# Three quarters of a down projection by Strassen's scheme on one core of a Trainium2

## The chip, the cores and the metric

The kernel runs on one core of one Trainium2 chip. The metric is device time in microseconds (us) of the whole program, smaller is better. Engines are named as in the profile: PE (TensorE matmuls), PEld (its weight loads), DVE (VectorE), ACT (ScalarE), POOL (GpSimd), SP (the queue that issues most DMAs).

## What is computed

One encoder block on 512 tokens (and 16 meta tokens) of width 2048: a mixer (short convolution and neighbourhood attention), then a squared-ReLU MLP with 8192 hidden columns. The change lies in the last product of the MLP.

```python
h_res = h_res + mix @ w_out[l]
h = rms_norm(h_res, norm2_g[l])
h_res = h_res + jnp.square(jax.nn.relu(h @ w_up[l])) @ w_down[l]     # (512, 8192) @ (8192, 2048)
out = rms_norm(h_res, final_norm_g)[:, N_META:]
```

All is float32. Every product is made of three float32r matmuls: an operand x is kept as hi + lo (hi is x rounded, lo is x - hi), and x*y is hi*hi + hi*lo + lo*hi.

## The kernel before

Stages in order: input projection with convolution and attention, output projection with the operands of the up projection, up projection, down projection, final norm. Weights come in slabs of 128 x 1024 (512 KB). `load` (L157) takes the next of three buffers named `raw` and issues the DMA on SP; `split` (L180) makes hi by an ACT cast (L182) and lo by a DVE subtraction (L183). SP, ACT, DVE and POOL each work through their instructions in program order, and a `raw` buffer is free again when what was loaded into it has been split.

**Up projection** (L741 to L782). It already goes by the Strassen-Winograd scheme: a product of 2 x 2 blocks with seven block products (table `PROD`) in place of eight. There are 32 outputs n (256 hidden columns each), four steps s for each n, and one slab for each step. A step holds two sums indices m; for each m there are 7 products of 3 matmuls of 128x256, so 42 matmuls in a step, the 21 of the first m ahead of the 21 of the second. The first three products use blocks of the slab as they are (buffers `q`, three of them), the other four use sums of blocks (`tsum`, two buffers, then `wsp`, three buffers). `up_slab` makes these sums on DVE (L747 to L749). The activation operands, seven blocks for each m and each as hi and lo, lie in `places`: m = 0 to 3 in `sobuf`, 4 and 5 in `xa_hi` and `xa_lo`, 6 and 7 in `xc`. `up_out` (L767) joins the products of one n (an ACT copy and six DVE instructions that read PSUM, L774 to L779), applies the squared ReLU on ACT, and writes the result to DRAM (`a_d`).

**Down projection** (L815 to L849). It goes in eight chunks of 1024 hidden rows, and in each chunk over four groups i of 512 output columns. For each i there are 8 x 4 x 3 = 96 matmuls of 128x512 (`mm3`, L632 to L635; 128 tokens stationary, 512 columns of weights moving), four slabs `dn` that are split as they are, and four DVE instructions (L845) that scale a PSUM bank and add it to `acc`. In the first group of a chunk four loads of `a_d` are split into `sobuf` (seven buffers of it).

Of the kernel before, what the change touches and what calls it, by code (L numbers as in the profile page):

```python
# [99 lines left out]
def hybrid_block_kernel(  # L100
# [56 lines left out]
    def load(src, name):  # L157
        raw = wring["raw"].next(name)
        wring["last"] = nc.sync.dma_start(raw, src)
        return raw  # L160
# [209 lines left out]
    xa_hi = xap.tile([P, 8, SEQ], F32R, name="xa_hi")  # L370
    xa_lo = xap.tile([P, 8, SEQ], F32R, name="xa_lo")
# [3 lines left out]
    def xc_tiles(pool, n):  # L375
        for i in range(n):
            f = len(xc2)
            hi = pool.tile([P, 2, SEQ], F32R, name=f"xc_hi{f}")
            lo = pool.tile([P, 2, SEQ], F32R, name=f"xc_lo{f}")
            xc2.append((hi, lo))  # L380
# [4 lines left out]
    with tc.tile_pool(name="at", bufs=1, side="left") as at:  # L385
# [18 lines left out]
        for p in range(NPAIR):  # L404
# [122 lines left out]
            split(xa_hi[:, p, :], xa_lo[:, p, :], o, scale=ag[:, p : p + 1])  # L527
# [89 lines left out]
    places += [[(0, 7, by7(flat(t)[:, :SW7]))] for t in (xa_hi, xa_lo)]  # L617
# [20 lines left out]
    xa = [(xa_hi[:, f, :], xa_lo[:, f, :]) for f in range(8)]  # L638
# [86 lines left out]
    a_d = [dram.tile([P, 4 * HT], F32, name=f"a_d{n}") for n in range(NG)]  # L725
# [15 lines left out]
    def up_slab(n, s):  # L741
        raw = load(w_up[n, s], f"up{n}_{s}")
        w, t = by4(raw), by4(TS.next())
        q_hi, q_lo = (by4(v, 3) for v in Q3.next())
        split(q_hi, q_lo, w[:, :, 1:4, :])
        b12 = free_ap(raw[:, 0:1], [[512, 2], [0, 2], [1, P]])
        nc.vector.tensor_tensor(t[:, :, 0:2, :], b12, w[:, :, 1:3, :], op=ALU.add)  # L747
        nc.vector.tensor_tensor(t[:, :, 2, :], t[:, :, 0, :], w[:, :, 2, :], op=ALU.add)
        nc.vector.tensor_tensor(t[:, :, 3, :], t[:, :, 2, :], w[:, :, 3, :], op=ALU.add)  # L749
        t_hi, t_lo = (by4(v) for v in part_tiles(f"up{n}_{s}"))  # L750
        split(t_hi, t_lo, t)
        return (q_hi, q_lo), (t_hi, t_lo)

    def up_step(bs, n, s):
        both = up_slab(n, s)
        for k in range(2):
            m = 2 * s + k
            for q, (sm, w, x, b, c) in PROD.items():
                o = bs[b][:, c * HT : (c + 1) * HT]
                h, l = (v[:, k, w, :] for v in both[sm])  # L760
                xh, xl = (operand[m][x][:, i, :] for i in range(2))
# [3 lines left out]
                nc.tensor.matmul(o, lhsT=l, rhs=xh, start=False, stop=m == NPR - 1, skip_group_check=True)  # L765

    def up_out(bs, n):  # L767


        e, u = E.next()  # L770
        e, u = (v.rearrange("p (s c) -> p s c", c=HT) for v in (e, u))
# [28 lines left out]
    xcp.release()  # L800
    xe.release()
    xap.release()
    wp2 = ctx.enter_context(tc.tile_pool(name="wp2", bufs=1, side="left"))
    wring["raw"] = Ring(*raw_slots(3, wp), *raw_slots(2, wp2))
    wring["split"] = Ring(*split_slots(3, wp), *split_slots(3, wp2))
    A = Ring(*[lambda name, i=i: part(sobuf, 2048, i) for i in range(7)])
    pf = ctx.enter_context(tc.tile_pool(name="pf", bufs=1, side="left"))
    gF = pf.tile([P, D], F32, name="gF")
    sq = pf.tile([P, NT, 5], F32, name="sq")
    junk = [pf.tile([P, 512], F32, name=f"junk{i}") for i in range(2)]  # L810

    QUART = {(1, 1): 0, (0, 0): 1, (1, 0): 2, (0, 1): 3}
    tags = ["mm", "aux"]
    turn = 0
    for ch in range(NCHUNK):  # L815
# [3 lines left out]
        if last:  # L819
            with tc.issue_after(wring["last"].ins):  # L820
                nc.sync.dma_start(gF, final_g.partition_broadcast(P))
        for i in range(3 if last else 4):
            bs = [bank(tags[turn], f"d{ch}_{i}_{t}") for t in range(NT)]
            turn ^= 1
            for s_ in range(0, FCH, 2):
                if i == 0:

                    n = 4 * ch + s_ // 2
                    both = A.next()
                    split(both[:, 0:1024], both[:, 1024:2048], load(a_d[n], f"a{n}"))  # L830
# [24 lines left out]
    for t in range(NT):  # L855
# [7 lines left out]
        for i in range(halves):  # L863
# [7 lines left out]
            nc.scalar.activation(junk[t % 2][:, :n], a, AF.Square, accum_out=sq[:, t, 3 + i : 4 + i])  # L871
            nc.vector.tensor_tensor(a, a, gF[:, 1536 + i * n : 1536 + (i + 1) * n], op=ALU.mult)
# [6 lines left out]
        for i in range(4):  # L879
# [5 lines left out]
            nc.sync.dma_start(out_v[t][:, :, i * 512 : (i + 1) * 512], o)  # L885

# [58 lines left out]
```

## Time and profile before

| what | value |
| --- | --- |
| median of 3 runs (lowest to highest) | 2155.45 us (2155.43 to 2155.64) |
| profiled execution | 2155.03 us, of which the traced span is 2153.3 us |
| up projection | about 800 to 1447 us of the span |
| down projection without its last group | about 1447 to 2122 us |
| PE busy over the span | 2141.1 us, 99% |

The span runs from the first to the last instruction of the trace. PE's busy time counts overlapping matmuls, so the rate of a stage is read from the distance between the starts of matmuls.

### The profile page before, as it was taken

What the parts mean: (1) busy time and instruction counts of PE and PEld (TensorE: products, weight loads), DVE (VectorE), ACT (ScalarE), POOL (GpSimd) and SP (SyncE); (2) the same over time, 40 slices, a digit from 0 to 9 for tenths busy, and PEclk for the clock granted to TensorE, in tenths of its full rate; (3) what the DMA queues carried; (4) which work ended last, traced back from release to release, by engine and by line L of the source; (5) the groups of instructions that cost most, each with busy time, mean ns of one, the idle gap of its engine ahead of it and who ended that gap; (6) DMA issues with size and microseconds to landing.
All of it is one profiled execution on the core that took longest, in us unless ns stands there. A gap on an engine that the chain in (4) does not pass through costs nothing.

```text
span 2153.3 us, 33207 instructions
## 1 busy us (share of the span) xinstructions
PE 2141.1 (99%) x13660; PEld 1954.4 (91%) x13660; DVE 1291.3 (60%) x2015; ACT 799.4 (37%) x1110; POOL 141.1 (7%) x256
## 2 busy tenths in 40 slices
PE   9999999999999999999999999999999999999998
PEld 8999999999988889999999999998888888888887
DVE  7776766343435569888888888874444343434434
ACT  6455544222212335544544544552222222222223
POOL 1332321001110000000000000000000000000001
PEclk9999999999999999999999999999999999999999
DMA  5332222222253334334334333356343333433422
GB/s 193 91 93 79 77 90 71 97 90 96 91 166 108 118 127 136 131 126 138 130 126 138 131 124 138 133 193 223 114 133 106 126 127 108 137 117 117 147 89 79
DMA packets 89997, 261.32 MB, mean 121 GB/s; under 512 B 25636, under 2 KB 25716, under 8 KB 88692
## 3 DMA queue, kind: packets, MB, share of 16 engines
q1 hardware_dynamic: 84660, 238.22, 33.9%
q10 hardware_dynamic: 4608, 16.78, 1.9%
q0 software_dynamic: 576, 4.19, 0.5%
q8 instruction: 107, 1.75, 0.3%
q14 instruction: 46, 0.38, 0.1%
HBM read 233.99 MB, written 25.17 MB: 120 GB/s over the span
## 4 chain that ended last, share of the span: by engine, by line
PE 98%; POOL 1%; SPq 0%; DMA 0%; ACT 0%; issue 0%; POOLq 0%; ACTq 0%; DVE 0%
PE d L633 10%; PE d L634 10%; PE d L635 10%; PE u L764 10%; PE u L765 10%; PE u L763 10%; PE mm_u L211 1%; PE mm_c L211 1%; PE mm_u L208 1%; PE mm_c L208 1%; PE mm_u L209 1%; PE mm_c L209 1%; PE mm_b L211 1%; PE mm_b L208 1%; PE mm_b L209 1%; PE o_a L635 1%
## 5 line engine op out<-in xcount | busy, mean ns | idle before, releaser
L633 PE MATMUL d<-wsp_dn,sobuf 128*128 128x512 f32 x992 | 385.9, 389 | 0.0
L634 PE MATMUL d<-wsp_dn,sobuf 128*128 128x512 f32 x992 | 385.9, 389 | 0.0
L635 PE MATMUL d<-wsp_dn,sobuf 128*128 128x512 f32 x992 | 385.9, 389 | 0.0
L183 DVE TENSOR_TENSOR wsp_dn<-raw_dn,wsp_dn 128x1024 fp32r<-128x1024 f32 x124 | 151.7, 1224 | 265.7 <-ACT wsp_dn L182 265.5
L182 ACT CAST wsp_dn<-raw_dn 128x1024 fp32r<-128x1024 f32 x124 | 130.7, 1054 | 377.4 <-PE d L635 367.7
L635 PEld LDWEIGHTS d<-wsp_dn,sobuf 128*128 128x128 f32 x992 | 186.2, 188 | 38.7
L633 PEld LDWEIGHTS d<-wsp_dn,sobuf 128*128 128x128 f32 x992 | 186.2, 188 | 38.7
L634 PEld LDWEIGHTS d<-wsp_dn,sobuf 128*128 128x128 f32 x992 | 186.2, 188 | 38.6
L182 ACT CAST q<-raw_up 128x768 fp32r<-128x768 f32 x128 | 106.9, 835 | 236.1 <-PE u L764 167.0
L183 DVE TENSOR_TENSOR wsp_up<-tsum,wsp_up 128x1024 fp32r<-128x1024 f32 x128 | 156.4, 1223 | 49.0 <-ACT wsp_up L182 45.0
L182 ACT CAST wsp_up<-tsum 128x1024 fp32r<-128x1024 f32 x128 | 134.3, 1050 | 69.9 <-PE u L765 64.6
L763 PE MATMUL u<-sobuf,wsp_up 128*128 128x256 f32 x512 | 145.0, 283 | 0.0
L764 PE MATMUL u<-sobuf,wsp_up 128*128 128x256 f32 x512 | 145.0, 283 | 0.0
L765 PE MATMUL u<-sobuf,wsp_up 128*128 128x256 f32 x512 | 144.6, 283 | 0.0
L183 DVE TENSOR_TENSOR q<-raw_up,q 128x768 fp32r<-128x768 f32 x128 | 122.4, 957 | 34.3 <-ACT q L182 34.2
L764 PE MATMUL u<-sobuf,q 128*128 128x256 f32 x384 | 108.7, 283 | 0.0
L763 PE MATMUL u<-sobuf,q 128*128 128x256 f32 x384 | 108.5, 283 | 0.0
L765 PE MATMUL u<-sobuf,q 128*128 128x256 f32 x384 | 108.5, 283 | 0.0
L183 DVE TENSOR_TENSOR sobuf<-raw_a,sobuf 128x1024 fp32r<-128x1024 f32 x32 | 39.2, 1225 | 103.2 <-ACT sobuf L182 103.2
L845 DVE SCALAR_TENSOR_TENSOR acc<-d,few,acc 128x512 f32<-128x512 f32 x124 | 86.2, 749 | 23.9 <-PE d L635 23.9
L763 PEld LDWEIGHTS u<-sobuf,wsp_up 128*128 128x128 f32 x512 | 98.3, 192 | 0.0
L764 PEld LDWEIGHTS u<-sobuf,wsp_up 128*128 128x128 f32 x512 | 98.3, 192 | 0.0
(307 smaller groups left out, 5466.7 us busy)
## 6 DMA issues: line engine op xcount, KB each, us to landing
raw_up<-in_w_up_dram SPq DMA_DIRECT2D x128, 512.0 KB
raw_dn<-in_w_down_dram SPq DMA_DIRECT2D x124, 512.0 KB
a_d<-xq ACTq DMA_DIRECT2D x32, 512.0 KB
raw_a<-a_d SPq DMA_DIRECT2D x32, 512.0 KB
raw_q<-in_w_in_dram SPq DMA_DIRECT2D x16, 512.0 KB
raw_u<-in_w_in_dram SPq DMA_DIRECT2D x16, 512.0 KB
raw_c<-in_w_in_dram SPq DMA_DIRECT2D x16, 512.0 KB
raw_b<-in_w_in_dram SPq DMA_DIRECT2D x16, 512.0 KB
```

What stands on the lines that cost most here:

```text
L182: first = nc.scalar.copy(hi, src)
L183: second = nc.vector.tensor_tensor(lo, src, hi.bitcast(F32), op=ALU.subtract)
L208: nc.tensor.matmul(b, lhsT=wh, rhs=cols(h_hi, kt), start=kt == 0, stop=False)
L209: nc.tensor.matmul(b, lhsT=wh, rhs=cols(h_lo, kt), start=False, stop=False)
L211: last = nc.tensor.matmul(b, lhsT=wl, rhs=cols(h_hi, kt), start=False, stop=kt == KT - 1)
L633: nc.tensor.matmul(o, lhsT=ah, rhs=wh, start=start, stop=False)
L634: nc.tensor.matmul(o, lhsT=ah, rhs=wl, start=False, stop=False)
L635: nc.tensor.matmul(o, lhsT=al, rhs=wh, start=False, stop=stop)
L763: nc.tensor.matmul(o, lhsT=h, rhs=xh, start=first, stop=False, skip_group_check=True)
L764: nc.tensor.matmul(o, lhsT=h, rhs=xl, start=False, stop=False, skip_group_check=True)
L765: nc.tensor.matmul(o, lhsT=l, rhs=xh, start=False, stop=m == NPR - 1, skip_group_check=True)
L845: nc.vector.scalar_tensor_tensor(a, bs[t], rs2[:, t : t + 1], a, op0=ALU.mult, op1=ALU.add)
```

## The change

The first 6144 of the 8192 hidden rows (`NPD` = 24 of the 32 outputs n) go through the down projection in the transposed Strassen form; the last 2048 stay in the old form, as chunks 6 and 7. The new part has four chunks `ch` of 1536 hidden rows (`CP` = 6 sums indices m). In each chunk there are eight groups G of 256 output columns; a group has three steps of one slab and 42 matmuls of 128x256, in which weights are stationary and activations move. So there are 4 x 8 x 3 = 96 steps.

- The sums of weight blocks of these steps are made by POOL instead of DVE (`step_slab` with `nc.gpsimd`): one instruction of 512 elements for each partition and two of 256.
- `up_out` has POOL make four sums of activation blocks (256 elements each) for the first 24 n, and writes them to DRAM too.
- `down_operand` loads the operands of one m in two parts (`da`, 768 columns, and `ds`, 1024 columns), through the same three `raw` buffers, and splits them into `places`, over the operands that were there. It is called inside the last group of the chunk before (and inside n = 31 of the up projection for chunk 0), two m after each step.
- A group ends in `combine_out` (an ACT copy and six DVE instructions). In chunk 0 that writes `accT`; in chunks 1 to 3 it writes a buffer that POOL adds to `accT` (one instruction of 1024 elements).
- In chunk 6 PE transposes `accT` back (64 transposes of 128x128), and 16 more DVE instructions add it to `acc`.

```diff
+    NPD = 24
+    xs = xap.tile([P, 4, HT], F32, tag="xa1", name="xs")
-    def up_slab(n, s):
-        raw = load(w_up[n, s], f"up{n}_{s}")
+    def step_slab(raw, eng, name):
         w, t = by4(raw), by4(TS.next())
         q_hi, q_lo = (by4(v, 3) for v in Q3.next())
         split(q_hi, q_lo, w[:, :, 1:4, :])
         b12 = free_ap(raw[:, 0:1], [[512, 2], [0, 2], [1, P]])
-        nc.vector.tensor_tensor(t[:, :, 0:2, :], b12, w[:, :, 1:3, :], op=ALU.add)
-        nc.vector.tensor_tensor(t[:, :, 2, :], t[:, :, 0, :], w[:, :, 2, :], op=ALU.add)
-        nc.vector.tensor_tensor(t[:, :, 3, :], t[:, :, 2, :], w[:, :, 3, :], op=ALU.add)
+        eng.tensor_tensor(t[:, :, 0:2, :], b12, w[:, :, 1:3, :], op=ALU.add)
+        eng.tensor_tensor(t[:, :, 2, :], t[:, :, 0, :], w[:, :, 2, :], op=ALU.add)
+        eng.tensor_tensor(t[:, :, 3, :], t[:, :, 2, :], w[:, :, 3, :], op=ALU.add)
...
+        if n < NPD:
+            nc.gpsimd.tensor_tensor(xs[:, 0, :], e[:, 0, :], e[:, 1, :], op=ALU.subtract)
+            nc.gpsimd.tensor_tensor(xs[:, 1, :], xs[:, 0, :], e[:, 2, :], op=ALU.subtract)
+            nc.gpsimd.tensor_tensor(xs[:, 2, :], e[:, 2, :], e[:, 0, :], op=ALU.subtract)
+            nc.gpsimd.tensor_tensor(xs[:, 3, :], e[:, 3, :], xs[:, 1, :], op=ALU.add)
+            nc.gpsimd.dma_start(a_d[n][:, 1024:], xs.rearrange("p s c -> p (s c)"))
+    CP = 6
+    def down_operand(n):
+        v = places[n % CP][0][2]
+        r = load(a_d[n][:, 256:1024], f"da{n}", 768)
+        split(v[:, 0:3, 0, :], v[:, 0:3, 1, :], by_q(r))
+        r = load(a_d[n][:, 1024:], f"ds{n}")
+        split(v[:, 3:7, 0, :], v[:, 3:7, 1, :], by_q(r))
...
             up_step(bs, n, s_)
+            if n == NG - 1 and s_ < 3:
+                for m in range(2 * s_, 2 * s_ + 2):
+                    down_operand(m)
         up_out(bs, n)
+    for ch in range(NPD // CP):
+        for G in range(8):
+            bs = banks(G)
+            for s_ in range(CP // 2):
+                name = f"dt{ch}_{G}_{s_}"
+                raw = wring["raw"].next(name)
+                for k in range(2):
+                    wring["last"] = nc.sync.dma_start(
+                        raw[:, k * 512 : (k + 1) * 512].rearrange("p (e c) -> p e c", e=2),
+                        w_down[G // 2, ch * CP + 2 * s_ + k].rearrange("p (e c) -> p e c", e=2)[:, :, G % 2 * 256 :][:, :, :256],
+                    )
+                step(bs, step_slab(raw, nc.gpsimd, name), ops_d, 2 * s_, CP)
+                if G == 7 and ch + 1 < NPD // CP:
+                    for m in range(2 * s_, 2 * s_ + 2):
+                        down_operand((ch + 1) * CP + m)
+            if ch == 0:
+                t = acc_pools[G].tile([P, 2, SEQ], F32, tag=f"xc_{('hi', 'lo')[G % 2]}{G // 2}", name=f"accT{G}")
+                accT.append(by_q(flat(t)))
+                combine_out(bs, accT[G], u_d)
+            else:
+                e = ED.next()
+                combine_out(bs, e, u_d)
+                nc.gpsimd.tensor_tensor(accT[G], accT[G], e, op=ALU.add)
...
-    for ch in range(NCHUNK):
+    for ch in range(first_ch, NCHUNK):
...
+                if ch == first_ch:
+                    pt = bank(tags[turn], f"pt{i}_{t}")
+                    for k in range(4):
+                        v = accT[2 * i + k // 2][:, QUART[t // 2, k % 2], t % 2 * P : (t % 2 + 1) * P]
+                        nc.tensor.transpose(pt[:, k * P : (k + 1) * P], in_=v, identity=ident)
+                    nc.vector.scalar_tensor_tensor(a, pt, rs2[:, t : t + 1], a, op0=ALU.mult, op1=ALU.add)
```

**Where instructions stand.** First SP at the end of the up projection. `raw_up31_1` is the slab of n = 31, step 1; `raw_a0` and `raw_dn0_0_0` are the first activations and weights of the down projection. Before:

```order
L159 DMA raw_up31_0_14773<-in_w_up_dram 128x1024
L159 DMA raw_up31_1_14825<-in_w_up_dram 128x1024
L159 DMA raw_up31_2_14877<-in_w_up_dram 128x1024
L159 DMA raw_up31_3_14929<-in_w_up_dram 128x1024
L159 DMA raw_a0_15012<-a_d0_7855 128x1024
L159 DMA raw_dn0_0_0_15016<-in_w_down_dram 128x1024
```

With the change, where `raw_da0` and `raw_ds0` are the two parts of the operands of m = 0:

```order
L159 DMA raw_up31_0_14895<-in_w_up_dram 128x1024
L159 DMA raw_da0_14947<-a_d0_7856 128x768
L159 DMA raw_ds0_14951<-a_d0_7856 128x1024
L159 DMA raw_da1_14955<-a_d1_7857 128x768
L159 DMA raw_ds1_14959<-a_d1_7857 128x1024
L159 DMA raw_up31_1_14963<-in_w_up_dram 128x1024
L159 DMA raw_da2_15015<-a_d2_7858 128x768
L159 DMA raw_ds2_15019<-a_d2_7858 128x1024
L159 DMA raw_da3_15023<-a_d3_7859 128x768
L159 DMA raw_ds3_15027<-a_d3_7859 128x1024
L159 DMA raw_up31_2_15031<-in_w_up_dram 128x1024
```

Four operand loads now stand between one slab and the next, and the next but one; the three `raw` buffers are taken in this order. SP shows the same pattern (`dt0_7_0`, four operand loads, `dt0_7_1`, four, `dt0_7_2`, four, `dt1_0_0`) at the end of each of chunks 0, 1 and 2.

Second DVE in chunk 0 at its last group, where before stood a slab's subtraction (`wsp_dn`) and the L845 instructions of the old form:

```order
L183 TENSOR_TENSOR sobuf_6589<-raw_ds6_16419,sobuf_6589 128x4x256
L183 TENSOR_TENSOR sobuf_6589<-raw_da7_16423,sobuf_6589 128x3x256
L183 TENSOR_TENSOR sobuf_6589<-raw_ds7_16427,sobuf_6589 128x4x256
L183 TENSOR_TENSOR q3_1_7852<-raw_dt0_7_1_16431,q3_1_7852 128x768
L183 TENSOR_TENSOR wsp_dt0_7_1_16439<-tsum_7851,wsp_dt0_7_1_16439 128x1024
L183 TENSOR_TENSOR sobuf_6589<-raw_da8_16484,sobuf_6589 128x3x256
L183 TENSOR_TENSOR sobuf_6589<-raw_ds8_16488,sobuf_6589 128x4x256
```

The subtractions for the operands of m = 0 and 1 of the next chunk stand ahead of those for the slab of the step that PE does next.

Third POOL in chunk 3 (in the down projection before, POOL had nothing until the final norm), around the sums of group 4:

```order
L750 TENSOR_TENSOR tsum_7851<-raw_dt3_4_0_20097 128x2x256
L751 TENSOR_TENSOR tsum_7851<-tsum_7851,raw_dt3_4_0_20097 128x2x128
L752 TENSOR_TENSOR tsum_7851<-tsum_7851,raw_dt3_4_0_20097 128x2x128
L750 TENSOR_TENSOR tsum_7851<-raw_dt3_4_1_20150 128x2x256
L860 TENSOR_TENSOR accT2_15666<-accT2_15666,xq_6617 128x1024
L751 TENSOR_TENSOR tsum_7851<-tsum_7851,raw_dt3_4_1_20150 128x2x128
```

The three sums of each slab and, once in a group, the addition to `accT` of two groups ago follow each other on POOL.

## Rows read from the trace of the kernel before

**Rows 1.** The page: busy time by engine, and the chain that ended last.
```profile
PE 2141.1 (99%) x13660; PEld 1954.4 (91%) x13660; DVE 1291.3 (60%) x2015; ACT 799.4 (37%) x1110; POOL 141.1 (7%) x256
...
PE 98%; POOL 1%; SPq 0%; DMA 0%; ACT 0%; issue 0%; POOLq 0%; ACTq 0%; DVE 0%
```

**Rows 2.** Windows (busy us and instructions by engine): up projection, then down projection.
```profile
801.00:1441.00 640.00, 640.00 (x5337) 640.00 (x5336) 538.04 (x844) 316.97 (x364) 0.53 (x1) 1.00 0.39 133
1441.00:2126.00 685.00, 685.00 (x3049) 568.31 (x3049) 284.53 (x299) 173.24 (x184) 5.18 (x12) 1.00 0.38 128
```

**Rows 3.** Waits between engines in the up, then the down projection: total, times, longest.
```profile
ACT q L182 <- PE u L764: 167.0, 94, 4.8
...
ACT wsp_dn L182 <- PE d L635: 367.7, 93, 4.4
```

**Rows 4.** PE's timeline late in the up projection: first and last of 78 matmuls.
```profile
1429.77 0.28 PE L763 MATMUL u<-sobuf,q 128*128 128x256 f32 x1
...
1439.01 0.28 PE L765 MATMUL u<-xa_hi,wsp_up 128*128 128x256 f32 x1
```

**Rows 5.** Down projection by tile: durations, first and last start.
```profile
L633 PE MATMUL d<-wsp_dn,sobuf x992: 389/389/396, 1447.4 to 2121.3; 128*128 128x512 f32 x199
...
L845 DVE SCALAR_TENSOR_TENSOR acc<-d,few,acc x124: 739/750/751, 1467.4 to 2122.8; 128x512 f32<-128x512 f32 x124
```

**Rows 6.** The chain in order of time: eight transposes by PE.
```profile
672.62 0.87 PE p2t L666 x8
```

**Rows 7.** Groups of the up projection: count, then busy us and mean ns.
```profile
L183 DVE TENSOR_TENSOR wsp_up<-tsum,wsp_up 128x1024 fp32r<-128x1024 f32 x128 | 156.4, 1223 | 49.0 <-ACT wsp_up L182 45.0
...
L182 ACT CAST wsp_up<-tsum 128x1024 fp32r<-128x1024 f32 x128 | 134.3, 1050 | 69.9 <-PE u L765 64.6 <-issue 2.6 <-PE o_c L635 1.4
...
L183 DVE TENSOR_TENSOR q<-raw_up,q 128x768 fp32r<-128x768 f32 x128 | 122.4, 957 | 34.3 <-ACT q L182 34.2
L182 ACT CAST q<-raw_up 128x768 fp32r<-128x768 f32 x128 | 106.9, 835 | 236.1 <-PE u L764 167.0 <-issue 58.5 <-DMA raw_up<-in_w_up_dram 10.5
...
L747 DVE TENSOR_TENSOR tsum<-raw_up 128x512 f32<-128x512 f32 x128 | 88.1, 689 | 4.1 <-DMA raw_up<-in_w_up_dram 1.3
...
L749 DVE TENSOR_TENSOR tsum<-tsum,raw_up 128x256 f32<-128x256 f32 x128 | 54.1, 423 | 2.9
L748 DVE TENSOR_TENSOR tsum<-tsum,raw_up 128x256 f32<-128x256 f32 x128 | 54.0, 423 | 2.8
```

**Rows 8.** Timelines of SP and ACT: one load and the cast that waited for it.
```profile
1504.38 0.33 SPq L159 DMA_DIRECT2D raw_a<-a_d  x1
...
1507.53 1.05 ACT L182 CAST sobuf<-raw_a 128x1024 fp32r<-128x1024 f32 x1 [4.44 <-DMA raw_a<-a_d]
```

**Rows 9.** POOL additions in the convolution (ns), then timelines of DVE beside them.
```profile
L549 POOL TENSOR_TENSOR ub<-ub,rs_bc x2: 641/694/746, 354.3 to 355.0; 128x258 f32<-128x258 f32 x1, 128x256 f32<-128x256 f32 x1
...
355.07 1.68 DVE L183 TENSOR_TENSOR wsp_b<-raw_b,wsp_b 128x1024 fp32r<-128x1024 f32 x1 [0.49 <-ACT wsp_b L182]
...
L549 POOL TENSOR_TENSOR ub<-ub,rs_bc x2: 743/1221/1699, 494.2 to 494.9; 128x258 f32<-128x258 f32 x1, 128x256 f32<-128x256 f32 x1
...
494.88 1.23 DVE L183 TENSOR_TENSOR wsp_b<-raw_b,wsp_b 128x1024 fp32r<-128x1024 f32 x1 [0.49 <-ACT wsp_b L182]
```

**Rows 10.** POOL's 512-element additions (ns), and DVE instructions beside one at 331.87.
```profile
L584 POOL TENSOR_TENSOR sqc<-sqc,zsq x7: 1283/1583/1584, 417.4 to 622.4; 128x512 f32<-128x512 f32 x7
...
331.87 1.34 POOL L533 TENSOR_TENSOR sqa<-sqa,ysq 128x512 f32<-128x512 f32 x1 [8.13 <-ACT ysq L532]
...
332.10 0.44 DVE L465 CUSTOM_DVE_ANT_0 s<-sp,s 128x272 f32<-128x272 f32 x1
```

**Rows 11.** PE's last matmul, then windows (PEclk is the third number from the right).
```profile
2143.95 0.28 PE L635 MATMUL dl<-wsp_dlast,sobuf 128*128 128x256 f32 x1
...
2145.50:2147.00 1.50, 0.00 (x0) 0.00 (x0) 0.70 (x2) 0.39 (x1) 0.97 (x2) 0.81 0.77 243
2147.00:2149.00 2.00, 0.00 (x0) 0.00 (x0) 0.49 (x2) 0.94 (x2) 0.00 (x0) 0.50 0.30 69
```

More of the change, by code (lines that the diff above doesn't have):

```diff
@@ L154, in hybrid_block_kernel, with load @@
     wring = {}
-    def load(src, name):
-        raw = wring["raw"].next(name)
+    def load(src, name, n=SLAB):
+        raw = wring["raw"].next(name)[:, :n]
         wring["last"] = nc.sync.dma_start(raw, src)
@@ L369, in hybrid_block_kernel @@
     xap = tc.alloc_tile_pool(name="xap", bufs=1, side="left")
-    xa_hi = xap.tile([P, 8, SEQ], F32R, name="xa_hi")
-    xa_lo = xap.tile([P, 8, SEQ], F32R, name="xa_lo")
+    xa7 = [xap.tile([P, 7, SEQ], F32R, tag=f"xa7_{i}", name=f"xa7_{i}") for i in range(2)]
+    xa1 = xap.tile([P, 2, SEQ], F32R, tag="xa1", name="xa1")
+    xa = [[t[:, f, :] for t in xa7] if f < 7 else [xa1[:, i, :] for i in range(2)] for f in range(8)]
     xe = tc.alloc_tile_pool(name="xe", bufs=1, side="left")
@@ L616, in hybrid_block_kernel @@
     places = [[(0, 7, by7(sobuf[:, m * SW7 : (m + 1) * SW7]))] for m in range(4)]
-    places += [[(0, 7, by7(flat(t)[:, :SW7]))] for t in (xa_hi, xa_lo)]
+    places += [[(0, 7, by7(flat(t)[:, :SW7]))] for t in xa7]
     spots = [by7(flat(t)) for both in xc2 for t in both][:7]
@@ L724, in hybrid_block_kernel @@
     E = Ring(*[lambda name, i=i: (part(flat(xq), 1024, i), ctmp[:, i, :]) for i in range(2)])
-    a_d = [dram.tile([P, 4 * HT], F32, name=f"a_d{n}") for n in range(NG)]
+    NPD = 24
+    a_d = [dram.tile([P, (8 if n < NPD else 4) * HT], F32, name=f"a_d{n}") for n in range(NG)]
+    xs = xap.tile([P, 4, HT], F32, tag="xa1", name="xs")
     PROD = {
@@ L760, in up_step @@
                 h, l = (v[:, k, w, :] for v in both[sm])
-                xh, xl = (operand[m][x][:, i, :] for i in range(2))
+                xh, xl = (ops[m][x][:, i, :] for i in range(2))
                 first = m == 0 and q in (1, 2, 3, 5)
@@ L764, in up_step, with combine_out @@
                 nc.tensor.matmul(o, lhsT=h, rhs=xl, start=False, stop=False, skip_group_check=True)
[L765 to L771, printed above, removed]
+                nc.tensor.matmul(o, lhsT=l, rhs=xh, start=False, stop=m == n - 1, skip_group_check=True)
+    def up_step(bs, n, s):
+        name = f"up{n}_{s}"
+        step(bs, step_slab(load(w_up[n, s], name), nc.vector, name), operand, 2 * s, NPR)
+    def combine_out(bs, e, u):
         two = lambda v: v.rearrange("p (a b) -> p a b", a=2)
@@ L795, in hybrid_block_kernel @@
             up_step(bs, n, s_)
+            if n == NG - 1 and s_ < 3:
+                for m in range(2 * s_, 2 * s_ + 2):
+                    down_operand(m)
         up_out(bs, n)
-    accs = acc_tiles()
[L800 to L805, printed above, removed]
+    acc_pools = [xe, xe] + [xcp] * 6
@@ new lines, in hybrid_block_kernel @@
+    accT = []
+    u_d = by_q(sqc)
+    ED = Ring(*[lambda name, i=i: by_q(part(flat(xq), 1024, i)) for i in range(2)])
+    for ch in range(NPD // CP):
[21 more added lines that the diff above has]
+                nc.gpsimd.tensor_tensor(accT[G], accT[G], e, op=ALU.add)
@@ L806, in hybrid_block_kernel @@
+    accs = acc_tiles()
+    raws = [part(flat(xq), 1024, i) for i in range(2)] + [flat(xap.tile([P, 2, SEQ], F32, tag="xa1", name="raw_x"))]
+    wring["raw"] = Ring(*raw_slots(3, wp), *[lambda name, v=v: v for v in raws])
+    more = [xap.tile([P, 7, SEQ], F32R, tag=f"xa7_{i}", name=f"wsp_x{i}") for i in range(2)]
+    wring["split"] = Ring(*split_slots(3, wp), *[lambda name, v=v: flat(v)[:, : 2 * SLAB] for v in more])
     A = Ring(*[lambda name, i=i: part(sobuf, 2048, i) for i in range(7)])
-    pf = ctx.enter_context(tc.tile_pool(name="pf", bufs=1, side="left"))
@@ L820, in hybrid_block_kernel @@
             with tc.issue_after(wring["last"].ins):
-                nc.sync.dma_start(gF, final_g.partition_broadcast(P))
+                for k in range(2):
+                    gF.append(flat(acc_pools[k].tile([P, 2, SEQ], F32, tag=("xc_hi0", "xc_lo0")[k], name=f"gF{k}")))
+                    nc.sync.dma_start(gF[k], final_g[k * 1024 : (k + 1) * 1024].partition_broadcast(P))
+            junk = xcp.tile([P, 2, SEQ], F32, tag="xc_hi1", name="junk")
         for i in range(3 if last else 4):
@@ L885, in hybrid_block_kernel @@
             nc.sync.dma_start(out_v[t][:, :, i * 512 : (i + 1) * 512], o)
+    xcp.release()
+    xe.release()
+    xap.release()
 def window_mask():
```

48 lines of the change are left out of this document (27 added, 21 removed).

## Prediction

> **What bounds the kernel now.** The page comes first: PE is busy for 99% of the span, and the chain that ended last is PE for 98% [rows 1]. The windows by stage say the same of the two stages at issue: PE never pauses in either [rows 2]. So what a stage takes is its count of matmuls times the distance between their starts. Late in the up projection 77 distances take 1439.01 - 1429.77 = 9.24 us, 0.120 us for a matmul of 128x256 [rows 4]. In the down projection the 992 rows of L633 are a third of 2976 matmuls, from 1447.4 to 2121.3: 673.9 / 2973 = 0.2267 us for one of 128x512 [rows 5]. The waits show why the other engines don't matter: ACT waits up to 4.8 and 4.4 us for PE to free a buffer [rows 3], so weights are ready before PE wants them. A change can win by fewer or shorter matmuls; it loses wherever weights or operands come later than PE.
>
> **What PE loses and gains.** Removed: three quarters of 8 x 4 x 96 matmuls, 2304 x 0.2267 = 522.3 us. Added: 96 steps x 42 = 4032 matmuls of the form of [rows 4], 483.8 us. Net -38.5 us. The 64 transposes cost 0.87 / 8 = 0.109 us each [rows 6]: +7.0 us. The 96 slab splits and 96 L845 instructions that go were beside PE: nothing.
>
> The 16 new additions take PSUM banks that the next group needs; each lasts 0.75 us [rows 5]. In a group eight of them (6 us) have to end, the first four beside PE's last matmuls, so the next group starts on some banks late, by about 1.5 us each time: +6 us (0 to 10).
>
> **The handover of operands: the largest term.** At four places (into chunk 0, and from each chunk to the next) a step's slab stands on SP behind four operand loads, and with three `raw` buffers it gets the one that `ds` of the step's first m had. That buffer is free only when PE has done this m, since the split overwrites what PE reads. So the slab for step s + 1 is asked for in the midst of step s, and PE has nothing else in its order. Time from the start of a step, whose two halves take 21 x 0.120 = 2.52 us each:
> - 2.52 PE is done with the first m; ACT casts `ds` (1.05), DVE subtracts (1.22) [rows 7]: 4.79.
> - The load is issued; a load of this size took 1507.53 - 1504.38 = 3.15 us to the cast that waited for it [rows 8]: 7.94.
> - On DVE the second m's `ds` is ahead. Its buffer was that of the first m's `da`, which is done after 12 matmuls (1.44), a cast (0.84) and a subtraction (0.96): 3.24, loaded 6.39, cast 7.44, subtracted 8.66.
> - POOL's first sum (1.28, the least of [rows 10]) can't run beside that subtraction (next part): 9.94. Then the slab's own subtraction on DVE (0.96), 10.90, and two more sums (0.64 each, the least of [rows 9]), 12.18; cast 13.23; subtraction 14.45, or 14.05 with the three overlaps of 0.13 us found below.
> - By then PE has done the nine matmuls that need no sums (1.08 us). So the step that starts anew began, as it were, at 14.05 - 1.08 = 12.97, not 5.04: 7.9 us lost.
>
> At the end of the up projection the sums are on DVE and take 0.69 + 0.42 + 0.42 [rows 7]: 8.66 + 1.53 + 1.05 + 1.22 - 1.08 = 11.38, 6.3 us lost. Three steps at each place: 9 x 7.9 + 3 x 6.3 = 90 us; before chunks 2 and 3 POOL's addition to `accT` (1024 elements, 2.57) also stands between the sums: +5. I take 95. Lower bound: no port conflict and sums as fast as DVE's, 7.94 + 1.53 + 1.05 + 1.22 - 1.08 - 5.04 = 5.6 a step, 67 us. Upper: 10 a step, if the slabs' shorter rows land later and POOL waits more between its sums, 120 us.
>
> **POOL and DVE beside each other.** In the first pair POOL's last addition runs 354.99 to 355.66; DVE's subtraction, which reads two SBUF tiles, starts at 355.07 and takes 1.68 us, not 1.22. In the second pair DVE came first, and POOL's addition took 1.70, not 0.64 [rows 9]. Yet a DVE instruction with one SBUF input keeps its 0.44 us beside POOL [rows 10]. The two together take 1.72 to 1.76 us where 1.22 + 0.64 = 1.86 would be one after the other: exclusion, less about 0.13 us.
>
> A group of a later chunk has three slabs: DVE's subtractions 3 x (0.96 + 1.22) = 6.54 us, POOL's 4096 elements 8 x 1.283 = 10.26 us. One after the other less six overlaps: 16.8 - 0.8 = 16.0, where PE needs 15.12: 0.9 us lost in each of 22 groups (three chunks, without the two last groups that the handover holds anyway), +20 us. In chunk 0, without `accT`'s addition, it is 14.2 and hidden. Bounds: 0, and 60 us if POOL's dependent sums leave gaps of half a microsecond.
>
> [...]
>
> **Smaller terms.** [...] Into chunk 6, a load of `a_d` waits for POOL's last addition: +3 (0 to 13). In the up projection DVE is busy 538 of 640 us, 16.95 of 20.16 for each n [rows 2]; POOL's four sums (4 x 0.64) may hold it up to 2.57, 19.5 in all, still hidden: 0 (to 13).
>
> **Sum.** -38.5 + 7 + 6 + 95 + 20 + 9 + 3 = +101.5. The profiled execution took 2155.03 us (its span 2153.3), 0.02% under the median of the runs: 2256.5, say 2257 us.
>
> **Rivals.**
> - *The handover alone.* If POOL's additions run more freely and the clock holds, the handover costs about 80 and nothing else is late: 2155 - 38.5 + 7 + 6 + 80 + 3 = 2212 us. For it: the overlap in [rows 9]. Against: no stretch of this trace has POOL and DVE both so loaded.
> - *POOL binds.* Port losses of 55, handover 105, clock 25, and 8 into chunk 6: 2155 - 38.5 + 7 + 10 + 105 + 55 + 25 + 8 = 2327 us. For it: POOL's additions took 1.58 us in the median, above the 1.28 used here [rows 10].
> - *The handover is hidden*, so the kernel gets faster: 2155 - 38.5 + 7 + 6 + 3 = 2133 us. That needs operands or slabs ahead of PE, under (38.5 - 16) / 12 = 1.9 us lost a step. Against: the cast that waits for PE, the subtraction and the load alone put the slab at 7.94, already 2.9 past 5.04.
>
> **How the numbers follow.** A difference of 0.2% (4.3 us) can be told from no change. Chances: my sum 0.58 (2225 to 2295), the handover alone 0.22 (2190 to 2225), POOL binds 0.15 (2295 to 2345), hidden 0.04, and 0.01 for a sum that ends within 0.2%. So faster 0.04, same 0.01, slower 0.95. The range from 2195 to 2320 takes in all of the first, nearly all of the second and half of the third: 0.85.
>
> **What would show it.** Right: the new stage's matmuls still start 0.120 us apart inside a step; PE idles at twelve steps, 5 to 8 us each, ended by the slab's subtraction after a chain cast, subtraction, load, sums; ACT's casts of `sobuf` and `xa7` wait for PE there; POOL and DVE together fill the groups of chunks 1 to 3, which take about 16 us, those of chunk 0 about 15.1. Wrong: matmuls of another pitch, slabs that are loaded before the operands' split, a handover step under 10 us, or groups of chunks 1 to 3 above 18 us.

## The result, and the profile after

The changed kernel takes 2265.47 us (median of 4 runs, 2264.47 to 2266.60), the kernel before 2155.44 beside it: 1.0511 times as long, 95% interval 1.0492 to 1.0529. The prediction was 2257 us with a range of 2195 to 2320.

The page after, to be read against [rows 1]: busy time by engine, PE's busy tenths and granted clock in 40 slices, and the chain that ended last.
```profile
PE 2159.6 (95%) x15452; PEld 2051.4 (91%) x15452; DVE 1548.5 (68%) x2247; ACT 901.2 (40%) x1262; POOL 705.3 (31%) x688
...
PE   9999999999999999999999999799698797898998
...
PEclk9999999999999999999999999899799798898999
...
PE 79%; POOL 9%; DMA 3%; DVE 3%; issue 3%; ACT 2%; SPq 1%; POOLq 0%; ACTq 0%; DVEq 0%
```
PE was 98% of the chain and is 79%. The dips in both strips stand at the same four places (called handovers below), where one chunk's operands are replaced by the next's. The waits of PE from the last column group of the up projection on (us in total, times, longest) say what it stands for there:
```profile
PE u L766 <- ACT q L182: 56.6, 12, 5.6
PE u L766 <- ACT wsp_dt L182: 21.7, 9, 6.3
...
PE u L768 <- DVE wsp_dt L183: 3.2, 5, 0.9
...
PE u L766 <- ACT wsp_up L182: 1.4, 2, 0.8
```
Twelve waits for `q`, the cast of a new slab: one for each of three steps at four places. The ACT timeline of the changed kernel shows both halves of the story, the evaluation of groups (L778) in chunk 0, a handover, and L778 in chunk 1:
```profile
1502.90 0.37 ACT L778 COPY sqc<-u 128x256 f32<-128x256 f32 x1 [0.19 <-ACT q L182]
1518.02 0.37 ACT L778 COPY sqc<-u 128x256 f32<-128x256 f32 x1 [0.77 <-PE u L768]
...
1587.70 0.83 ACT L182 CAST q<-raw_dt 128x768 fp32r<-128x768 f32 x1 [1.12 <-DMA raw_dt<-in_w_down_dram]
1591.29 1.04 ACT L182 CAST wsp_dt<-tsum 128x1024 fp32r<-128x1024 f32 x1 [2.76 <-POOL tsum L752]
...
1602.33 0.83 ACT L182 CAST q<-raw_dt 128x768 fp32r<-128x768 f32 x1 [1.07 <-DMA raw_dt<-in_w_down_dram]
1605.92 1.04 ACT L182 CAST wsp_dt<-tsum 128x1024 fp32r<-128x1024 f32 x1 [2.76 <-POOL tsum L752]
...
1641.75 0.37 ACT L778 COPY sqc<-u 128x256 f32<-128x256 f32 x1
1657.76 0.36 ACT L778 COPY sqc<-u 128x256 f32<-128x256 f32 x1
```
A group of chunk 0 takes 15.12 us and L778 waits for PE; in chunk 1 ACT comes by every 16.0 us and waits for nobody: the preparation of slabs is the slower one there. In the handover the two casts of sums are 14.63 us apart, where a step of PE is 5.04. SP's timeline has the slab loads that belong to these casts:
```profile
1583.48 1.21 SPq L845 DMA_DIRECT2D raw_dt<-in_w_down_dram  x2
...
1597.78 1.20 SPq L845 DMA_DIRECT2D raw_dt<-in_w_down_dram  x2
```
From issue to the cast is 4.22 and 4.55 us; the load of [rows 8] took 3.15. The two loads differ in form: a slab is issued as two DMAs of 256 KB, which takes SP 1.21 us, that of [rows 8] as one in 0.33. PE's timeline in the first of the two steps:
```profile
1588.58 0.58 PE L766 MATMUL u<-sobuf,q 128*128 128x256 f32 x1 [5.13 <-ACT q L182]
...
1592.39 0.58 PE L766 MATMUL u<-sobuf,wsp_dt 128*128 128x256 f32 x1 [1.46 <-ACT wsp_dt L182]
1592.77 0.42 PE L767 MATMUL u<-sobuf,wsp_dt 128*128 128x256 f32 x1
1592.98 0.41 PE L766 MATMUL u<-sobuf,wsp_dt 128*128 128x256 f32 x1
...
1598.36 0.28 PE L767 MATMUL u<-sobuf,wsp_dt 128*128 128x256 f32 x1
1598.47 0.28 PE L768 MATMUL u<-sobuf,wsp_dt 128*128 128x256 f32 x1
```
Behind these waits matmuls start 0.21 us apart, with the granted clock at 0.50 from 1588 to 1592 us, and 0.12 again only near the step's end, with 1.00 from 1597.5 to 1598.5. Windows (busy us and instructions of PE, PEld, DVE, ACT, POOL, then granted clock, DMA share, GB/s) of the handover into chunk 1, of chunk 1 behind it, and of the start of chunk 6:
```profile
1578.40:1639.00 60.60, 39.53 (x247) 38.04 (x246) 36.23 (x37) 23.63 (x27) 25.48 (x21) 0.75 0.46 148
1639.00:1731.50 92.50, 91.91 (x766) 91.70 (x765) 70.82 (x71) 32.59 (x41) 82.92 (x58) 1.00 0.32 100
...
2058.80:2122.00 63.20, 54.56 (x237) 44.17 (x236) 28.58 (x35) 15.14 (x16) 2.39 (x1) 0.89 0.62 225
```

**Where the 111.5 us of span went.** From the start of the last up group (1428.4) to the first matmul of chunk 6 (2058.9) are 630.5 us, for 168 + 4032 matmuls that take 504.0 at 0.120. So 126.5 us are lost in this stage: 83.4 us of waits (the four rows above and 0.5 for one more), and 43.1 us in which PE counts as busy; of these some 37 us lie in matmuls that start 0.15 to 0.39 us apart, as those of the step above do (granted clock 0.50). The groups between handovers have only 1.9 us of it (0.59 + 0.64 + 0.64, waits of L768), so the handovers cost about 125. With -38.5 for the matmuls, +1.1 up to the up projection (its first `u` matmul starts at 801.70, not 800.56), and +0.5 at the end, 21.9 us are left for chunks 6 and 7: -38.5 + 1.1 + 126.5 + 0.5 + 21.9 = 111.5.

### The profile page after: what moved, and what is told of

The parts are those of the page before. It is cut to its first block, busy times and chain, and to the rows that moved or that the text cites. A ratio compares the mean times of both kernels' runs of the same rounds, so it can differ in the third digit from the quotient of the medians.

```text
span 2264.8 us, 38337 instructions
## 1 busy us (share of the span) xinstructions
PE 2159.6 (95%) x15452; PEld 2051.4 (91%) x15452; DVE 1548.5 (68%) x2247; ACT 901.2 (40%) x1262; POOL 705.3 (31%) x688
## 3 DMA queue, kind: packets, MB, share of 16 engines
q0 software_dynamic: 4032, 16.78, 1.9%
## 4 chain that ended last, share of the span: by engine, by line
PE 79%; POOL 9%; DMA 3%; DVE 3%; issue 3%; ACT 2%; SPq 1%; POOLq 0%; ACTq 0%; DVEq 0%
PE u L766 13%; PE u L767 13%; PE u L768 13%; POOL tsum L750 4%; POOL tsum L751 2%; PE d L634 2%; PE d L635 2%; PE d L636 2%; DMA raw_dt<-in_w_down_dram 1%; PE mm_u L211 1%; PE mm_c L211 1%; PE mm_u L208 1%; PE mm_c L208 1%; PE mm_u L209 1%; PE mm_c L209 1%
## 5 line engine op out<-in xcount | busy, mean ns | idle before, releaser
L766 PE MATMUL u<-sobuf,q 128*128 128x256 f32 x768 | 223.8, 292 | 35.1 <-ACT q L182 35.1
L750 POOL TENSOR_TENSOR tsum<-raw_dt 128x512 f32<-128x512 f32 x96 | 158.5, 1651 | 295.7 <-DMA raw_dt<-in_w_down_dram 236.5
L183 DVE TENSOR_TENSOR wsp_dt<-tsum,wsp_dt 128x1024 fp32r<-128x1024 f32 x96 | 148.9, 1551 | 116.3 <-ACT wsp_dt L182 116.0
L767 PE MATMUL u<-sobuf,q 128*128 128x256 f32 x768 | 222.7, 290 | 0.0
L768 PE MATMUL u<-sobuf,q 128*128 128x256 f32 x768 | 219.3, 290 | 0.5 <-DVE q L183 0.5
L182 ACT CAST wsp_dt<-tsum 128x1024 fp32r<-128x1024 f32 x96 | 100.8, 1050 | 252.3 <-POOL tsum L752 246.7
L766 PEld LDWEIGHTS u<-sobuf,q 128*128 128x128 f32 x768 | 152.9, 199 | 36.5 <-ACT q L182 36.5
L766 PE MATMUL u<-sobuf,wsp_dt 128*128 128x256 f32 x512 | 149.8, 293 | 17.3 <-ACT wsp_dt L182 17.3
L183 DVE TENSOR_TENSOR q<-raw_dt,q 128x768 fp32r<-128x768 f32 x96 | 148.9, 1551 | 24.0 <-ACT q L182 23.9
L767 PEld LDWEIGHTS u<-sobuf,q 128*128 128x128 f32 x768 | 153.2, 199 | 0.0
L768 PEld LDWEIGHTS u<-sobuf,q 128*128 128x128 f32 x768 | 150.5, 198 | 1.1 <-DVE q L183 1.1
L768 PE MATMUL u<-sobuf,wsp_dt 128*128 128x256 f32 x512 | 145.6, 291 | 3.2 <-DVE wsp_dt L183 3.2
L767 PE MATMUL u<-sobuf,wsp_dt 128*128 128x256 f32 x512 | 148.6, 290 | 0.0
L183 DVE TENSOR_TENSOR q<-raw_up,q 128x768 fp32r<-128x768 f32 x128 | 134.0, 1047 | 17.0 <-ACT q L182 16.8
L768 PE MATMUL u<-sobuf,wsp_up 128*128 128x256 f32 x512 | 144.6, 284 | 0.0
L797 POOL TENSOR_TENSOR xs<-xq 128x256 f32<-128x256 f32 x24 | 22.9, 953 | 358.5 <-ACT xq L792 355.3
L766 PE MATMUL u<-xa,q 128*128 128x256 f32 x384 | 112.0, 292 | 17.3 <-ACT q L182 17.3
```

The costliest lines, as they stand in the source:

```text
L182: first = nc.scalar.copy(hi, src)
L183: second = nc.vector.tensor_tensor(lo, src, hi.bitcast(F32), op=ALU.subtract)
L750: eng.tensor_tensor(t[:, :, 0:2, :], b12, w[:, :, 1:3, :], op=ALU.add)
L768: nc.tensor.matmul(o, lhsT=l, rhs=xh, start=False, stop=m == n - 1, skip_group_check=True)
```

## The experiments

The theory: the handovers are the loss, because a slab's load stands behind the loads of operands in three buffers; GpSimd's sums make groups of 16.0 us, but PE lives on slabs that were prepared while it stood in a handover. The rivals: the bound is GpSimd, or the exclusion between its instructions and VectorE's that [rows 9] show (the recorded texts call it the port); or it is the clock.

Most kernels below ran once. Ten runs of one of them lie within 4.8 us, and up to the first `u` matmul, where the kernels hardly differ, the profiled executions took from 801.3 to 805.1 us; a difference of a few us between single runs is no finding.

**Without operand loads.**
```
-                if G == 7 and ch + 1 < NPD // CP:
+                if G == 7 and ch + 1 < 0:
```


> The three handovers inside the down part are taken away: the operands of k-blocks 6 to 23 are not loaded (chunks 1 to 3 multiply those of chunk 0 again, so the output is that of other data); every slab, sum, matmul and accumulation stays. Theory 'handover': the three handovers cost 101.3 us together in the changed kernel, so 2265.5 - 101 = 2164 us is left if nothing else waits. But the store of prepared slabs that hid the 16.0 us cadence of the groups is built in the handovers, so without them the deficit of 0.88 us in each of 24 groups should come through, less what the store of chunk 0 covers (some 9 us): 2173 to 2179 us. Rival 'the port never binds': 2164 us, groups at 15.12 us all through. Rival 'GpSimd binds and the handovers only hide it': over 2200 us, since a group would take more than 16.5 us.

Measured: 2177.25 us. The second run adds this:
```
-                step(bs, step_slab(raw, nc.gpsimd, name), ops_d, 2 * s_, CP)
+                step(bs, step_slab(raw, nc.vector, name), ops_d, 2 * s_, CP)
```


> As the run without operand loads (output of other data), and the three sums of every slab run on VectorE as in the up projection; only the accumulation of a group stays on GpSimd. Theory 'handover': GpSimd and the port have no part left, all 32 groups at 15.12 us, 2162 to 2166 us. The difference to the run that keeps the sums on GpSimd is the price of the sums there: 9 to 15 us by this theory, 0 by the rival 'the port never binds', over 35 us by 'GpSimd binds'.

Measured: 2157.78 us, below the range expected. ACT's timeline without operand loads, sums on GpSimd:
```profile
1849.83 0.36 ACT L778 COPY sqc<-u 128x256 f32<-128x256 f32 x1
1865.84 0.36 ACT L778 COPY sqc<-u 128x256 f32<-128x256 f32 x1
```
and with sums on VectorE:
```profile
1852.35 0.38 ACT L778 COPY sqc<-u 128x256 f32<-128x256 f32 x1 [0.73 <-PE u L768]
1867.47 0.38 ACT L778 COPY sqc<-u 128x256 f32<-128x256 f32 x1 [0.73 <-PE u L768]
```
The first is in the range that only the theory gave: with the handovers gone, the 16.0 us cadence comes through, and it goes with the sums. The difference is 19.5 us, above the 9 to 15 expected. 1.8 us of it lie ahead of the first `u` matmul (805.1 and 803.3), where nothing was changed; from there to the last `u` matmul it is 11.9 us, and what follows is 5.8 us shorter, 17.7 in all. I had left out that late sums also hold back the loads of chunk 6: its first weight load was issued 11.4 us ahead of the last `u` matmul, and 17.9 us ahead with the sums on VectorE.

**All sums on VectorE, handovers as they are** (the second edit above alone).

> The changed kernel with the sums of every slab on VectorE, handovers as they are. Theory 'handover': a handover step loses the 3.3 us of GpSimd's sums and gets some 1.2 us of VectorE's for them, so 12 steps give back some 2 us each: 2235 to 2245 us, 20 to 30 us less than the changed kernel; PE still idles at twelve steps. Rival 'GpSimd or the port is the main loss': 2155 to 2185 us, most of the 110 us gone. Rival 'nothing of it is GpSimd': 2263 to 2268 us.

Measured: 2251.63 us, 14 less than the changed kernel: a miss, between theory and "nothing". The stage ends 7.4 us earlier (2051.4 for 2058.8) and the rest is 7.6 us shorter (198.4 of span behind that matmul, not 206.0). In this execution the first `u` matmul came 3.1 us later than in the changed kernel's (804.8, not 801.7), so behind it some 18 us were saved, still short of 20. Its ACT timeline in a handover:
```profile
1593.68 1.04 ACT L182 CAST wsp_dt<-tsum 128x1024 fp32r<-128x1024 f32 x1 [1.82 <-DVE tsum L752]
...
1607.84 1.04 ACT L182 CAST wsp_dt<-tsum 128x1024 fp32r<-128x1024 f32 x1 [1.88 <-DVE tsum L752]
```
The wait for the sums falls from 2.76 to 1.85 us, but the steps are still 14.16 us apart instead of 14.63. In this step the loads take back about half of what the sums give: the second slab's load took 4.96 us to its cast, not 4.55.

**Slabs three steps ahead.** `make` loads and prepares the next slab in order and puts it into `made`; three are made before the first step.
```
-                step(bs, step_slab(raw, nc.gpsimd, name), ops_d, 2 * s_, CP)
...
+                step(bs, made.pop(0), ops_d, 2 * s_, CP)
+                make()
                 if G == 7 and ch + 1 < NPD // CP:
```


> The same work, but each slab is loaded and prepared three steps ahead in the program, so that in a handover the load of a slab stands ahead of the loads of the operands on SyncE's queue, and its casts and sums ahead of theirs. Theory 'the slab is late because it stands behind the operands': a handover falls from 31 to 36 us to 10 to 15 us, what its 12 operand casts and subtractions need beside three slabs; 2175 to 2200 us. Rival 'the operands themselves are late' (their loads, through three buffers, are what PE waits for, whatever stands first): no more than 20 us less than the changed kernel, 2245 us or above.

Measured: 2216.17 us, 49 less, between the two. PE's waits for `q` are gone from the head of the list; in their place it waits for the operands' own casts and subtractions (`sobuf`, `xa`), 22.8 us in 21 waits, and for `wsp_dt`, 12.9 us in five. So the place in the order is worth 49 of the handovers' 125 us; what is left goes with operands and slabs together, and this run does not part the two.

**Groups interleaved on either side of a handover.** In place of A's three steps, then B's: A0 B0 A1 B1 A2 B2, so an operand is free for longer. Four kernels: as it is; with a fourth buffer (the first line below); with this buffer and two of three sums on VectorE; with this buffer and all of them there.
```
+    wring["raw"] = Ring(*raw_slots(3, wp), lambda name: flat(xs))
...
+    runs = [(0, 1), (2,), (3,), (4,), (5,), (6, 7)]
+    todo += [(ch, G, s_) for ch in range(NPD // CP) for run in runs for s_ in range(NS) for G in run]
```


> As the run with the slabs three steps ahead, and the two groups on either side of a handover are interleaved (first k-pair of both, second of both, third of both; likewise the last two column groups of the up projection), so that an operand is free for 10 us instead of 5 before the next pair of steps and is wanted again 20 us later. Same instructions. Theory 'handover': the four handovers fall to 0 to 5 us each, and the deficit of 0.88 us in 24 groups, which the run without operand loads priced at 19.5 us, now comes through: 2150 to 2168 us. Rival 'the operands come too slowly through three buffers, however they are ordered': 2190 us or more. Rival 'the deficit stays hidden': 2140 us.

> The interleaved kernel with a fourth buffer for loads in the down part (the 4 KB tile of the up projection's sums, free by then). Theory 'handover': if loads still hold a handover back, 5 to 15 us less than with three buffers; if the handovers are already hidden, within 2 us of it.

> The interleaved kernel with four buffers, and of the three sums of a slab only the first (512 elements) on GpSimd, the other two on VectorE. A group then asks GpSimd for about 3 x 1.7 + 3.4 = 8.5 us of 15.12. Theory 'handover plus a deficit by GpSimd's sums': the deficit is gone, 2138 to 2148 us, below the kernel before (2155). Rival 'VectorE is the bound in the handovers': 2150 us or more.

> The interleaved kernel with four buffers and all sums on VectorE. By the run without operand loads (2157.8 us, which still has the first handover, some 20 us) this leaves 2138 to 2145 us if the interleaved handovers cost nothing; that is 10 to 17 us below the kernel before: the matmul term of -38.5 less chunk 6's 21.8 and a few us. Rival 'VectorE is the bound in the handovers' (6 operands of 2.2 us of subtractions beside 6 slabs of about 4 us in 30 us): 2148 to 2165 us.

Measured: 2216.45, 2183.97, 2184.24 and 2157.51 us (the last in 10 runs, 2155.14 to 2159.95; ratio to before 1.0004, interval 0.9994 to 1.0014). None is where the theory had it; the first is in the range of the rival that three buffers are too few, the last two in that of the rival VectorE. The order alone brings nothing, the fourth buffer 32 us, the move of all sums 26, the move of two of three nothing. PE's waits in the first:
```profile
PE u L766 <- DVE xq L783: 14.8, 8, 3.6
PE u L766 <- ACT wsp_dt L182: 13.4, 8, 2.4
```
The interleaving brought a wait of its own: L783 evaluates the group that has just ended, and the next group needs its PSUM banks. With all sums on VectorE (windows of chunk 0 and of chunk 1, then a row of VectorE's timeline and one of GpSimd's):
```profile
1465.00:1570.00 105.00, 105.00 (x877) 105.00 (x876) 93.03 (x150) 47.41 (x56) 0.00 (x0) 1.00 0.42 135
...
1600.00:1680.00 80.00, 80.00 (x669) 80.00 (x668) 78.61 (x118) 33.55 (x41) 27.24 (x6) 1.00 0.33 105
```
```profile
1675.68 3.17 DVE L183 TENSOR_TENSOR q<-raw_dt,q 128x768 fp32r<-128x768 f32 x1
```
```profile
1675.58 2.46 POOL L880 TENSOR_TENSOR accT<-accT,xq 128x1024 f32<-128x1024 f32 x1 [11.93 <-DVE xq L784]
```
VectorE has no slack left in chunk 1, and in chunk 0 it has: what differs is GpSimd's accumulation, beside which one subtraction of `q` took 3.17 us instead of 0.95. Why two of three sums on VectorE gave nothing stays open. PE's waits in that stage are 33.8 us there, 23.7 of them for L783; they are 32.0 and 17.2 with all sums on GpSimd, 14.9 and 8.5 with all on VectorE. L750 waited most, 198 us in all, for VectorE's last subtraction to release one of the two `tsum` buffers, but no run changed their number.

**No additions on GpSimd in the new steps.** The kernel with four buffers and all sums on VectorE, with pairs as A0 B0 A1 A2 B1 B2, a separate buffer for one part of the operands, the evaluation of a group given priority in the order of instructions, and:
```
-            nc.gpsimd.tensor_tensor(accT[G], accT[G], e, op=ALU.add)
+            nc.gpsimd.dma_start(accT[G], e, accum_op=ALU.add)
```


> The interleaved kernel with all sums on VectorE, and three edits for what its trace showed: the interleaved pairs run as A0 B0 A1 A2 B1 B2, so that the results of A leave their banks 10 us before they are wanted instead of 5 (its PE waited 4.3 us at two handovers for L783); a buffer of their own for the loads of three of the seven operand parts; and the accumulation of a group's result by an accumulating DMA instead of GpSimd's 3.4 us (beside which VectorE's subtraction of q took 3.2 us instead of 0.95). In the interleaved kernel VectorE was busy 78.6 of 80 us in the groups of chunk 1, and 93.0 of 105 us in chunk 0, where nothing is accumulated. Theory 'VectorE is what is left of the handover': 2136 to 2148 us, below the kernel before. Rival 'the load of operands still binds' (buffers and queue): 2150 to 2160 us as the interleaved kernel. Rival 'the accumulating DMA is slow or in the way': over 2160 us.

Measured: 2148.53 us in 5 runs (2145.18 to 2150.30), before 2155.62: 0.9960, interval 0.9947 to 0.9974. It is the one version that beats both kernels, the kernel before by 0.4%; just outside the range given. The edits were made together, so what each of them brought of the 9 us isn't shown. PE's waits, and the window of chunk 2's 121 us:
```profile
PE d L634 <- ACT sobuf L182: 13.8, 1, 13.8
PE u L769 <- ACT wsp_dt L182: 3.4, 3, 2.1
```
```profile
1694.00:1815.00 121.00, 119.92 (x1000) 119.72 (x999) 110.03 (x180) 56.72 (x69) 6.87 (x8) 1.00 0.65 185
```
The handovers cost 3.4 us of waits, not 83. What is left is one wait of 13.8 us at the start of chunk 6, for a load of `a_d` into `xq`. Rows of SP and ACT:
```profile
1948.51 0.33 SPq L159 DMA_DIRECT2D xq<-in_w_down_dram  x1
...
1958.60 1.05 ACT L182 CAST wsp_dn<-xq 128x1024 fp32r<-128x1024 f32 x1 [10.42 <-DMA xq<-in_w_down_dram]
...
1961.76 0.33 SPq L159 DMA_DIRECT2D xq<-a_d  x1
```
The last accumulating DMA, issued at 1949.38, reads from the same `xq`. The chain that ended last goes another way: a weight load took 10 us to its cast, the next weight load waited on SP for the split of it, and the load of `a_d` stands behind that one. Whether this wait could be had as well was not tried.

**Filling the waits.** 32 matmuls of a zero weight ahead of each handover step; in the second kernel 16 more ahead of the matmuls that wait for `wsp_dt`.
```
+    def fill(bs, n):
+        for _ in range(n):
+            nc.tensor.matmul(bs[0][:, :HT].rearrange("p (a b) -> p a b", a=2), lhsT=zr, rhs=free_ap(zr[:, 0:1], [[0, 2], [1, P]]), start=False, stop=False, skip_group_check=True)
```


> The changed kernel with 32 matmuls of a zero weight into an accumulating bank (they add nothing to it) ahead of each of the twelve steps of the handovers, 3.8 us at full clock in a wait of 4.1 to 5.6 us, so that TensorE works through most of the wait. In the changed kernel a handover's step runs its 42 matmuls at a pitch of 0.213 us instead of 0.120 (granted clock 0.5). Theory 'a part of the handover is the clock that falls in its waits': the steps run at 0.120 again, up to 3.6 us in each of 12, 2220 to 2240 us. Rival 'the waits alone set the handover' (the clock is hidden behind the loads of the next step): 2255 to 2268 us. Rival 'the clock falls anyway, and the extra matmuls only hold the step back': 2270 us or more.

> The changed kernel with zero-weight matmuls in both waits of each handover step: 32 ahead of the step, as in the run before this, and 16 more behind its first nine matmuls, ahead of those that wait for the cast of the sums. In the run with the first 32 alone the time stayed (2264.1 us): the first nine matmuls ran at 0.120, but the wait of 1.8 us behind them brought the clock down again, and the next 20 or so matmuls ran at 0.213 to 0.214, as in the changed kernel. Theory 'a part of the handover is the clock behind the wait for the sums': with that wait filled these run at 0.120, some 2 us less per step, and the next operands' casts, which wait for TensorE, come 1 to 2 us earlier: 2240 to 2254 us. Rival 'the loads alone set the handover': 2258 to 2268 us although all 42 matmuls of a step run at 0.120.

Measured: 2264.11 and 2268.07 us. PE's timeline with the second:
```profile
1592.91 2.08 PE L798 MATMUL u<-zr 128*128 128x256 f32 x16
1594.93 0.39 PE L770 MATMUL u<-sobuf,wsp_dt 128*128 128x256 f32 x1
1595.15 0.28 PE L771 MATMUL u<-sobuf,wsp_dt 128*128 128x256 f32 x1
1595.27 0.29 PE L770 MATMUL u<-sobuf,wsp_dt 128*128 128x256 f32 x1
```
and its window of the handover (PE alone, clock, DMA):
```profile
1578.00:1639.00 61.00, 52.10 (x405) 0.97 0.46 143
```
The clock was held at 0.97 instead of 0.75, the step's matmuls started 0.12 us apart, and the time did not fall. The casts of sums are at 1593.83 and 1608.56, 14.73 us apart. PE was done earlier, but the second slab's load, issued at 1599.68, took 5.29 us to its cast at 1604.97, with the next operand's load issued 1.3 us behind it instead of 1.8. So the rival holds, within the few us by which runs differ: the some 37 us of slow matmuls lie beside loads that the next step waits for anyway.

**Chunk 6 without the transposes** (the block of `pt` at L913 to L918 left out).

> The changed kernel without the 64 transposes of the accumulated three quarters into chunk 6 and the accumulation of them (so the output is the last quarter's alone); nothing else changes. Chunk 6 and 7 take 21.8 us more in the changed kernel than before. Theory of the prediction: 7.0 us of transposes and some 6 us of waits for their banks: 2250 to 2254 us. Rival 'the 21.8 us are the start of chunk 6 (loads of a, the clock)': 2257 to 2259 us, the transposes alone.

Measured: 2252.61 us, 12.9 less, as the prediction's two terms say. Behind the last `u` matmul alone it is 15.4 us (190.6 of span, not 206.0): this execution came to that matmul 1.4 us later than the changed kernel's profiled one, which itself lies 1.1 us above its median.

## Why the prediction held, by its steps

The sum came within 9 us of the measured time, and this is in part luck: handover and clock were 21 us too low and chunk 6 was 6 too low, while the term for POOL and VectorE beside each other was 18 too high.

- **Matmuls.** The pitch is 0.120 us wherever PE doesn't come out of a wait; -38.5 stands.
- **Handover, +95, with the clock +9.** The mechanism is the predicted one: in the first step of the place shown above the slab's load was issued 5.1 us after the step's start at 1578.40 (4.79 in the working), its sums came last, and PE resumed at 14.0 (14.05). Together the two terms were 104 and measured 125. Two things were mis-sized. A slab's load took 4.2 us and more to its cast (5.2 the longest with operand loads about it), not the 3.15 of [rows 8]. About 0.6 of the difference is that its second DMA is issued that much later. What stretches the rest isn't shown: with the next operand's load issued 3.0 us behind it instead of 1.3 a slab's load took 4.18, not 4.22, and one with no load behind it took 3.79. And the third step of a place, with which SP asks for three slabs in a row, waits longest (for `wsp_dt` up to 6.3 us). The times of a step hold for the first of a place; in the next one the slow matmuls lie ahead of the slab's load, which was issued 9.2 us after the step's first matmul. One detail was wrong: PE starts a step on the cast of `q`, not on VectorE's subtraction, since the nine matmuls of its first part are ordered with those of the low half last.
- **Clock, +9.** No run shows this term; it was an estimate of mine, and [rows 11] show the clock behind PE's last matmul alone. What the runs show in its place: in the step shown above 33 of 42 matmuls start 0.21 us apart instead of 0.12 (granted clock 0.50 from 1588 to 1592 us), and some 37 us are lost so in all, four times the term; but the two fill runs (0.89 and 0.97 over the handover into chunk 1, where it was 0.75) show that taking this away gives nothing back that single runs can tell. So 9 was too much as a price and far too little as an amount, and the sum of waits and slow matmuls must not be read as two prices.
- **POOL and VectorE beside each other, +20.** The cadence was right, 16.0 against 15.12. The step that failed was that it costs PE 0.9 us a group. Slabs stand ready when a chunk starts, as PE's standing still in the handover let preparation catch up, and the deficit of 0.88 x 8 = 7 us a chunk is paid from them: 1.9 us were seen, so PE's groups did not take the 16 us forecast. A further 7.6 us come at chunk 6, where the last loads are late, as the run with all sums on VectorE shows. Without operand loads the same deficit cost 17.7 us. So 20 was about the price of the cause when nothing else stops PE; here the larger loss hid half of it. That the two exclude each other but for a small overlap shows again: in the interleaved kernel with all sums on VectorE the subtraction that took 3.17 us began 0.10 behind an addition of 2.46, and 2.46 + 0.95 would be 3.41 from the addition's start, where 3.27 were seen. What lies behind it, a port or something else, no run shows.
- **Chunk 6, +7 +6 +3.** 21.9 measured. The transposes and their banks are 12.9 to 15.4 (predicted 13); what was taken for +3 is mostly the lateness of the last sums, 7.6. The two were taken from separate single runs and need not add up to the whole.
- **The rivals.** "The handover alone" would need the handovers at 80; "POOL binds" needed losses of 55 from POOL and VectorE beside each other and 25 from the clock, which no run shows, and all of GpSimd's sums are worth 14 to 18. "Hidden" needed slabs and operands ahead of PE, and this is what the last interleaved kernel does, at 2148.5: it takes another order of steps, two more buffers, all sums on VectorE, and an accumulation by DMA.

## What to carry to other kernels

When a shorter matmul schedule keeps its operands in place for a whole chunk, count what it costs to replace them: PE alone was to gain 38.5 us here, and twelve steps in which a load, two casts and three sums stand one behind the other cost three times that. A deficit of one engine and a stall of another didn't add here (the deficit cost 1.9 us between the handovers and 7.6 at chunk 6, but 17.7 without operand loads): the stall builds the store that pays for the deficit, so whoever removes the stall must remove the deficit too. And slow matmuls next to a wait (granted clock 0.50, some 37 us here) were no price that single runs can tell, as the next step waited for its loads in the same time: fill the wait and see.

## What the runs showed of the hardware that was not expected

- Also where only the wait inside a step was left unfilled (1.8 us in the step looked at, in the first of the fill runs), the next 22 or so matmuls started 0.21 us apart, with the granted clock at 0.57 from 1592 to 1598 us.
- With matmuls of a zero weight in both waits of a step the granted clock was 0.97 over the handover into chunk 1, with those ahead of the steps alone 0.89, and 0.75 in the changed kernel.
- An accumulating DMA of 512 KB took GpSimd 0.86 us to issue (6.87 us for the eight in the window of chunk 2), where an addition by GpSimd took 2.34 to 3.40 us in the changed kernel; beside one of 3.39 us there, a subtraction of `q` on VectorE took 3.15 us.
